# Finer first loads of x, transposes two blocks ahead, and filter tables on another queue in an encoder block on one core

## The chip, the cores and the metric

The kernel runs on one NeuronCore of a Trainium2 chip. The metric is device time in microseconds (us). Three timed runs of the kernel before took 2923.29, 2925.0 and 2925.0 us, median 2925.0. The engines are named as the profile names them: PE (matrix products; PEld its weight loads), DVE (vector), ACT (scalar), POOL (general), and SP, which only issues transfers. SP and ACT issue on hardware queues, POOL on a software queue.

## The reference

One block on x of 512 tokens x 2048 features, float32. Only its start matters here:

```
hn = rmsnorm(x, norm1_w)                     # x * rsqrt(mean(x*x) + eps) * w
proj = hn @ w_in                             # 2048 x 13328
conv_out = depthwise_conv(proj[..., :5120], conv_w, conv_b)     # 3 taps along the tokens
h = sin(f1 * (z @ w1 + b1)); h = sin(f2 * (h @ w2 + b2)); h = h @ w3   # filters of the long convolution
```

Behind it come the long convolutions by spectra (the tables c_dft), a chunked mLSTM in both directions whose gates are 16 columns of proj, the merge of both branches, and a gated feed-forward part.

## The kernel before

Every float32 operand of a product is split into a rounded part h and a remainder l (helper `split_w`, L160 to 166: ACT casts h, DVE subtracts), and a product is three PE passes, h·h, h·l and l·h (`mm3`, L72). Weights come in units of 128 x 4 x 256 (512 KB) through three buffers `wr`, loaded on SP (`load_a`, L154), and are split in two steps of two 128-row blocks each.

x is loaded as token rows (tiles `xt`, 128 tokens each) and must be transposed: for each of 16 blocks of 128 features, four PE transposes fill one PSUM bank (L280), ACT scales it by norm1_w into h (L283) and DVE makes l (L284). Both read norm1_w as a column, from the tile `cols`: conv_w, conv_b, norm1_w and norm2_w are loaded as rows (`rows_a`, `rows_b`, L97 to 102, on ACT's queue), transposed on PE (L105, L106) and copied by DVE (L107). Norm1's factor per token is applied later, after the products: the squares of x run on ACT (L291), their sums become `rstd` and the broadcast row `rbc` (L292 to 295).

The first group of w_in (256 columns, 16 blocks, `group_feat`, L192) is interleaved with this in the code: four blocks are transposed and split, then two steps of the group follow, a step being two blocks' products, 12 on PE (L275 to 287). Behind it come the gates' columns (tiles `wg`, four narrow loads of 128 x 4 x 16, L410 to 437, through the same `wr` and `wh` buffers), the second group, and so on. A side stream runs beside the groups: first `filter_net` (L526), which loads the tables c_dft and zt and the filter net's small weights and vectors on POOL's queue, splits the tables, and computes the net.

The order in the code is not the order of an engine: a scheduler at build time takes instructions from the code by its own estimates of when their operands are ready, and writes an order for each engine. An engine then works strictly in that order, waiting for semaphores. Transfers of the hardware queues take eight completion semaphores in turn, so an issue waits until the transfer eight issues earlier has landed. A buffer is loaded anew when its last readers are done; the pool `ph`, which holds the filter net's small tiles, lies where `xp` (x tiles, rows_a, rows_b) lay.

Of the kernel before, what the change touches and what calls it, by code (L numbers as in the profile page):

```python
# [34 lines left out]
def hybrid_block_kernel(ctx, tc, x, norm1_w, w_in, conv_w, conv_b, filt_w1, filt_b1, filt_freq1,  # L35
# [15 lines left out]

    cp = ctx.enter_context(tc.tile_pool(name="cp", bufs=1))
# [5 lines left out]
    ap = ap_cm.__enter__()  # L58
# [25 lines left out]

    csm = new(cp, "csm", (P, 3 * P + 16))
    nc.sync.dma_start(csm[:, 0:P], c_small[:, 0:P])
    nc.gpsimd.dma_start(csm[:, P:3 * P + 16], c_small[:, P:3 * P + 16])
    ident = csm[:, 0:P]
    triu = csm[:, P:2 * P]
    tril = csm[:, 2 * P:3 * P]  # L90
# [4 lines left out]
    xp_cm = tc.tile_pool(name="xp", bufs=1)  # L95
    xp = xp_cm.__enter__()
    rows_a = new(xp, "rows_a", (120, P))  # L97
    nc.scalar.dma_start(rows_a, conv_w[0].rearrange("k (b p) -> (k b) p", p=P))
    rows_b = new(xp, "rows_b", (72, P))
    nc.scalar.dma_start(rows_b[0:40], conv_b[0].rearrange("(b p) -> b p", p=P))  # L100
    nc.scalar.dma_start(rows_b[40:56], norm1_w[0].rearrange("(b p) -> b p", p=P))
    nc.scalar.dma_start(rows_b[56:72], norm2_w[0].rearrange("(b p) -> b p", p=P))
    cols = new(cp, "cols", (P, 192))
    pt = sd_ps()
    nc.tensor.transpose(pt[:, 0:120], rows_a, ident[0:120, 0:120])  # L105
    nc.tensor.transpose(pt[:, 120:192], rows_b, ident[0:72, 0:72])  # L106
    nc.vector.tensor_copy(cols, pt[:, 0:192])  # L107
    cw = cols[:, 0:120].rearrange("p (k b) -> p k b", k=3)
    cb = cols[:, 120:160]
    n1 = cols[:, 160:176]  # L110
    n2 = cols[:, 176:192]


    def dram(name, shape=(P, L)):
# [39 lines left out]
    def load_a(w, r0, c0, nk=4, ncol=256):  # L154
        n_tile[0] += 1
        raw = wpool[0].tile([P, nk, ncol], F32, tag="wr", name=f"wr_{n_tile[0]}", bufs=3)
        nc.sync.dma_start(raw, w[r0:r0 + nk * P, c0:c0 + ncol].rearrange("(k p) c -> p k c", p=P))
        return raw
# [33 lines left out]
    def group_feat(w, r0, nkb, c0, act, raws=None, ahead=None):  # L192

        ps = [mm_ps(), mm_ps()]
        units = w_units(w, r0, nkb, c0, raws)
        for u in range(0, nkb, 2):
            h, l = next(units) if ahead is None else ahead.get(c0, u)
            for j in range(2):
                for k in range(2):
                    kb = u + k  # L200
                    aH, aL = act[kb]
                    cs = slice(j * P, (j + 1) * P)
                    mm3(ps[j], h[:, k, cs], l[:, k, cs], aH, aL, kb == 0, kb == nkb - 1)
            yield None
        yield ps
# [57 lines left out]


    X = [None] * KB
    ssq_c = new(cp, "ssq_c", (P, 4, 4))
    xt = [[new(xp, f"xt{c}_{tb}") for tb in range(4)] for c in range(4)]
    raws = []
    for c in range(4):
        for tb in range(4):  # L270
            nc.sync.dma_start(xt[c][tb], x2d[tb * P:(tb + 1) * P, c * L:(c + 1) * L])
        if c < 3:
            raws.append(load_a(w_in, c * L, 0))
    first_group = group_feat(w_in, 0, KB, 0, X, raws)
    for c in range(4):  # L275
        for k in range(4):
            kb = 4 * c + k
            ps = sd_ps()
            for tb in range(4):
                nc.tensor.transpose(ps[:, tb * P:(tb + 1) * P], xt[c][tb][:, k * P:(k + 1) * P], ident)  # L280
            h = new(ap, "a", dt=F32R)
            l = new(ap, "a", dt=F32R)
            nc.scalar.activation(h, ps, AF.Copy, scale=n1[:, kb:kb + 1])  # L283
            nc.vector.scalar_tensor_tensor(l, ps, n1[:, kb:kb + 1], h.bitcast(F32), ALU.mult, ALU.subtract)  # L284
            X[kb] = (h, l)
        next(first_group)
        next(first_group)
    for c in range(4):
        for tb in range(4):
            sq = xp.tile([P, L], F32, tag="sq", name=f"sq{c}_{tb}", bufs=2)  # L290
            nc.scalar.activation(sq, xt[c][tb], AF.Square, accum_out=ssq_c[:, tb, c:c + 1])  # L291
    ssq = new(cp, "ssq", (P, 4))  # L292
    nc.vector.tensor_reduce(ssq, ssq_c, mybir.AxisListType.X, ALU.add)
    rstd = rstd_from(ssq, "n1")
# [10 lines left out]
    def gt(dt=F32, shape=(P, L)):  # L305
        t = vt(dt)[:, 0:2, 0:258].rearrange("p b c -> p (b c)")[:, 0:L]
        return t if len(shape) == 2 else t.rearrange("p (b c) -> p b c", b=shape[1])
# [218 lines left out]
    def filter_net():  # L526
        tables = []
        for m in range(4):
            t = gt()
            nc.gpsimd.dma_start(t, c_dft[m])  # L530
            tables.append(t)
        vec = new(ph, "fvec", (P, 4))
        for j, src in enumerate((filt_b1, filt_freq1, filt_b2, filt_freq2)):
            for half in range(2):
                nc.gpsimd.dma_start(vec[half * 64:half * 64 + 64, j:j + 1], src[0].rearrange("(n o) -> n o", o=1))
        w1 = new(ph, "fw1", (33, 2, 64))
        w2 = new(ph, "fw2", (64, 2, 64))
        for half in range(2):
            nc.gpsimd.dma_start(w1[:, half, :], filt_w1[0])
            nc.gpsimd.dma_start(w2[:, half, :], filt_w2[0])  # L540
        zt = gt()
        nc.gpsimd.dma_start(zt[0:33], c_zt)
        yield "pause"
        for m, t in enumerate(tables):
            hh = new(ph, f"dH{m}", dt=F32R)
            ll = new(ph, f"dL{m}", dt=F32R)
            nc.scalar.copy(hh, t)
            nc.vector.tensor_tensor(ll, t, hh.bitcast(F32), ALU.subtract)
            dft.append((hh, ll))
            yield 1  # L550
        def sin_layer(ps, b, fr):
            a = gt()
            nc.vector.tensor_scalar(a, ps, b, fr, ALU.add, ALU.mult)
            n = gt()
            nc.vector.tensor_scalar(n, a, INV2PI, MAGIC, ALU.mult, ALU.add)
            nc.vector.tensor_scalar(n, n, MAGIC, None, ALU.subtract)
            for c in (PI_A, PI_B, PI_C):
                nc.vector.scalar_tensor_tensor(a, n, -c, a, ALU.mult, ALU.add)
            nc.vector.tensor_scalar(a, a, PI_CLAMP, -PI_CLAMP, ALU.min, ALU.max)
            nc.scalar.activation(a, a, AF.Sin)  # L560
            return a
# [12 lines left out]
        nc.vector.tensor_tensor(h2["L"], hh, h2["H"].bitcast(F32), ALU.subtract)  # L574
        yield 4
# [755 lines left out]
    w2 = {t: cm.__enter__() for t, cm in w2_cm.items()}  # L1331
# [42 lines left out]
    xp = ctx.enter_context(tc.tile_pool(name="xd", bufs=1, reuse_waits="tile"))  # L1374
# [49 lines left out]
    for c in range(4):  # L1424
        t = new(xq, "xst")
# [14 lines left out]
    for tb in range(4):  # L1440
        ts = slice(tb * P, (tb + 1) * P)
        for c in range(4):
            ps = mm_ps()
            for k in range(NL):
                mm3(ps, H(k)[0][:, ts], H(k)[1][:, ts], W[(c, k)][0], W[(c, k)][1], k == 0, k == NL - 1)
            t = x2[tb][c]
            nc.vector.scalar_tensor_tensor(t, ps, norm2["r"][:, tb:tb + 1], t, ALU.mult, ALU.add)
            n_tile[0] += 1
            sq = xq.tile([P, L], F32, tag="sq", name=f"sq_{n_tile[0]}", bufs=2)
# [4 lines left out]
        for c in range(4):  # L1454
            t = x2[tb][c]
# [64 lines left out]
```

## Time and profile before

| | |
|---|---|
| timed runs, median | 2925.0 us (2923.29 to 2925.0) |
| profiled execution | 2923.41 us, of it span 2921.3 us |
| mean granted clock | 0.996 |
| PE busy | 2883.2 us, 99% of the span |
| DVE, ACT, POOL busy | 2112.2, 1272.4, 195.5 us |
| moved by DMA | 377.01 MB, mean 129 GB/s |

The span runs from the first to the last instruction that was recorded; the profiled execution's time is 2.1 us more. Busy shares are means over the whole span. A row of a timeline merges like instructions that follow each other; the bracket at its end is idle time of that engine before it, with what ended it.

### The profile page before, as it was taken

The page shows a single profiled execution, that of the slowest core. Times are in us where ns is not written, and L with a number is a line of the kernel's source. Part 1 is how long each engine was busy: PE and PEld are TensorE (multiplying, and loading weights), DVE is VectorE, ACT ScalarE, POOL GpSimd, SP SyncE. Part 2 cuts the span into 40 slices and gives each one's busy share as a digit, 9 for nine tenths or more (in the row PEclk, how much of TensorE's full clock was granted, in tenths as well). Part 3 has the DMA queues.
Part 4 walks back from the last instruction along what each step waited for, and adds up shares of the span by engine and source line. Part 5 has one row for each costly group of instructions (what it writes and reads, how often), then busy time and mean ns, then how long its engine had stood idle before and what let it go on. Part 6 is the DMA issues. An engine that isn't in the chain of part 4 may idle for free.

```text
span 2921.3 us, 48184 instructions
## 1 busy us (share of the span) xinstructions
PE 2883.2 (99%) x18412; PEld 2611.4 (89%) x18412; DVE 2112.2 (72%) x3843; ACT 1272.4 (44%) x2259; POOL 195.5 (7%) x449
## 2 busy tenths in 40 slices
PE   8999999999999999999999999999999999999998
PEld 6788887898889999888889999999999998888886
DVE  6897977889478888554449888888888885233336
ACT  5434354436564455222445444444444444233224
POOL 1101011102210001000110000000000000000000
PEclk9999999999999999999999999999999999999999
DMA  5334334334434444743443334333433336343433
GB/s 177 115 107 133 118 117 138 109 115 139 148 124 130 128 137 137 250 140 98 150 136 116 116 117 127 112 116 118 124 121 113 113 94 223 95 127 117 130 109 130
DMA packets 284161, 377.01 MB, mean 129 GB/s; under 512 B 18013, under 2 KB 221147, under 8 KB 283929
## 3 DMA queue, kind: packets, MB, share of 16 engines
q1 hardware_dynamic: 258976, 296.99, 33.1%
q0 software_dynamic: 23552, 74.74, 7.6%
q8 instruction: 144, 2.36, 0.3%
q10 hardware_dynamic: 1401, 2.20, 0.2%
q14 instruction: 88, 0.72, 0.1%
HBM read 326.67 MB, written 47.20 MB: 128 GB/s over the span
## 4 chain that ended last, share of the span: by engine, by line
PE 93%; DVE 3%; DMA 2%; issue 1%; ACT 1%; POOL 0%; SPq 0%; ACTq 0%; DVEq 0%; POOLq 0%
PE mm L70 67%; PE sd L70 26%; DMA wr<-in_w_down_dram 1%; DVE wl L165 0%; DMA xt<-in_x_dram 0%; DVE st L353 0%; PE sd L703 0%; PE sd L1279 0%; PE sd L280 0%; DVE h L81 0%; DMA g<-d_q 0%; DMA d_yb<-g 0%; DMA g<-d_hy 0%; DVE st L350 0%; DVE T L1307 0%
## 5 line engine op out<-in xcount | busy, mean ns | idle before, releaser
L165 DVE TENSOR_TENSOR wl<-wr,wh 128x512 fp32r<-128x512 f32 x512 | 351.1, 689 | 494.5 <-ACT wh L164 489.1
L164 ACT CAST wh<-wr 128x512 fp32r<-128x512 f32 x512 | 316.8, 622 | 768.8 <-PE mm L70 716.1
L70 PE MATMUL mm<-a,wh 128*128 128x512 f32 (+1 forms) x2136 | 625.6, 376 | 0.4 <-ACT wh L1025 0.4
L70 PE MATMUL mm<-T,h 128*128 128x256 f32 x2592 | 470.4, 284 | 3.9 <-ACT h L1025 3.9
L70 PE MATMUL sd<-T,h 128*128 128x256 f32 x2592 | 468.2, 283 | 0.0
L70 PEld LDWEIGHTS mm<-a,wh 128*128 128x128 f32 x2136 | 387.6, 190 | 70.8 <-issue 3.4
L70 PEld LDWEIGHTS mm<-T,h 128*128 128x128 f32 x2592 | 405.5, 193 | 4.3 <-ACT h L1025 4.3
L70 PEld LDWEIGHTS sd<-T,h 128*128 128x128 f32 x2592 | 404.4, 192 | 0.0
L70 PE MATMUL mm<-a,wl 128*128 128x512 f32 (+1 forms) x1068 | 399.8, 375 | 1.5 <-DVE wl L165 1.0
L70 PE MATMUL mm<-wh,h 128*128 128x512 f32 x1280 | 396.3, 391 | 3.7 <-ACT h L80 3.7
L1025 ACT CAST h<-s 128x512 fp32r<-128x512 f32 x395 | 244.8, 621 | 285.4 <-PE sd L70 141.9
L70 PE MATMUL mm<-T,l 128*128 128x256 f32 x1296 | 367.5, 284 | 0.8 <-DVE l L1026 0.8
L70 PE MATMUL sd<-T,l 128*128 128x256 f32 x1296 | 366.8, 283 | 0.0
L70 PEld LDWEIGHTS mm<-wh,h 128*128 128x128 f32 x1280 | 241.5, 189 | 54.3 <-ACT h L80 3.9
L1026 DVE TENSOR_TENSOR l<-s,h 128x512 fp32r<-128x512 f32 x395 | 270.6, 686 | 12.1 <-ACT h L1025 9.7
L1025 ACT CAST h<-r 128x512 fp32r<-128x512 f32 x285 | 176.8, 620 | 221.4 <-PE mm L70 111.2
L70 PE MATMUL mm<-wh,a 128*128 128x256 f32 (+1 forms) x1152 | 259.7, 319 | 0.0
L70 PEld LDWEIGHTS mm<-T,l 128*128 128x128 f32 x1296 | 249.5, 193 | 1.2 <-DVE l L1026 1.2
L70 PE MATMUL mm<-wl,h 128*128 128x512 f32 x640 | 250.0, 391 | 0.0
L70 PEld LDWEIGHTS sd<-T,l 128*128 128x128 f32 x1296 | 248.8, 192 | 0.0
L70 PEld LDWEIGHTS mm<-a,wl 128*128 128x128 f32 x1068 | 202.2, 189 | 37.3 <-DVE wl L165 1.9
L1026 DVE TENSOR_TENSOR l<-r,h 128x512 fp32r<-128x512 f32 x285 | 192.1, 688 | 51.9 <-ACT h L1025 51.6
(371 smaller groups left out, 4370.2 us busy)
## 6 DMA issues: line engine op xcount, KB each, us to landing
r<-in_w_gate_up_dram SPq DMA_DIRECT2D x176, 512.0 KB, 4.8
wr<-in_w_in_dram SPq DMA_DIRECT2D x144, 512.0 KB, 3.9
wr<-in_w_down_dram SPq DMA_DIRECT2D x88, 512.0 KB, 3.6
r<-in_w_in_dram SPq DMA_DIRECT2D x32, 512.0 KB, 4.8
wr<-in_w_out_dram SPq DMA_DIRECT2D x32, 512.0 KB, 5.4
d_h<-xo POOLq DMA_DIRECT2D x44, 256.0 KB, 2.6
hl<-d_h SPq DMA_DIRECT2D x44, 256.0 KB, 3.5
d_g<-xo POOLq DMA_DIRECT2D x32, 256.0 KB, 3.9
```

The source lines that it names most:

```text
L70: nc.tensor.matmul(o, a, b, start=start, stop=stop)
L164: nc.scalar.copy(h, src)
L165: nc.vector.tensor_tensor(l, src, h.bitcast(F32), ALU.subtract)
L1025: nc.scalar.copy(h, a)
L1026: nc.vector.tensor_tensor(l, a, h.bitcast(F32), ALU.subtract)
```

## The change

Four edits. x is loaded in five pieces of 256, 256, 512, 512 and 512 columns instead of four of 512, the first weights behind the first piece. The loop takes two blocks at a time: both are transposed, then one step of the group's products on the two blocks before them is emitted, then the two new blocks are split. The column constants are divided: norm1, norm2 and conv_b as `rows_b` with norm1 first, transposed after the first two blocks; conv_w as `rows_a`, loaded on SP and transposed after the first group. The loads of `filter_net` and the rest of c_small go from POOL's queue to SP's.

```diff
     nc.sync.dma_start(csm[:, 0:P], c_small[:, 0:P])
-    nc.gpsimd.dma_start(csm[:, P:3 * P + 16], c_small[:, P:3 * P + 16])
...
-    nc.scalar.dma_start(rows_a, conv_w[0].rearrange("k (b p) -> (k b) p", p=P))
     rows_b = new(xp, "rows_b", (72, P))
-    nc.scalar.dma_start(rows_b[0:40], conv_b[0].rearrange("(b p) -> b p", p=P))
-    nc.scalar.dma_start(rows_b[40:56], norm1_w[0].rearrange("(b p) -> b p", p=P))
-    nc.scalar.dma_start(rows_b[56:72], norm2_w[0].rearrange("(b p) -> b p", p=P))
+    nc.scalar.dma_start(rows_b[0:16], norm1_w[0].rearrange("(b p) -> b p", p=P))
+    nc.scalar.dma_start(rows_b[16:32], norm2_w[0].rearrange("(b p) -> b p", p=P))
+    nc.scalar.dma_start(rows_b[32:72], conv_b[0].rearrange("(b p) -> b p", p=P))
...
+    def small_columns():
+        pt = sd_ps()
+        nc.tensor.transpose(pt[:, 120:192], rows_b, ident[0:72, 0:72])
+        nc.vector.tensor_copy(cols[:, 120:192], pt[:, 120:192])
+
+    def conv_columns():
+        nc.sync.dma_start(rows_a, conv_w[0].rearrange("k (b p) -> (k b) p", p=P))
+        pt = sd_ps()
+        nc.tensor.transpose(pt[:, 0:120], rows_a, ident[0:120, 0:120])
+        nc.vector.tensor_copy(cols[:, 0:120], pt[:, 0:120])
...
-    xt = [[new(xp, f"xt{c}_{tb}") for tb in range(4)] for c in range(4)]
+    pieces = [(0, 256), (256, 256), (512, 512), (1024, 512), (1536, 512)]
+    xt = [[new(xp, f"xt{c}_{tb}", (P, n)) for tb in range(4)] for c, (_, n) in enumerate(pieces)]
     raws = []
-    for c in range(4):
+    for c, (c0, n) in enumerate(pieces):
         for tb in range(4):
-            nc.sync.dma_start(xt[c][tb], x2d[tb * P:(tb + 1) * P, c * L:(c + 1) * L])
-        if c < 3:
-            raws.append(load_a(w_in, c * L, 0))
+            nc.sync.dma_start(xt[c][tb], x2d[tb * P:(tb + 1) * P, c0:c0 + n])
+        if c in (0, 2, 3):
+            raws.append(load_a(w_in, len(raws) * L, 0))
...
+    for kb in range(0, KB, 2):
+        blocks = [x_block(kb), x_block(kb + 1)]
+        if kb == 0:
+            small_columns()
+        if kb:
+            next(first_group)
+        for k in range(2):
+            x_split(kb + k, blocks[k])
+    next(first_group)
+    conv_columns()
...
-            nc.gpsimd.dma_start(t, c_dft[m])
+            nc.sync.dma_start(t, c_dft[m])
...
-                nc.gpsimd.dma_start(vec[half * 64:half * 64 + 64, j:j + 1], src[0].rearrange("(n o) -> n o", o=1))
+                nc.sync.dma_start(vec[half * 64:half * 64 + 64, j:j + 1], src[0].rearrange("(n o) -> n o", o=1))
...
-            nc.gpsimd.dma_start(w1[:, half, :], filt_w1[0])
-            nc.gpsimd.dma_start(w2[:, half, :], filt_w2[0])
+            nc.sync.dma_start(w1[:, half, :], filt_w1[0])
+            nc.sync.dma_start(w2[:, half, :], filt_w2[0])
...
-        nc.gpsimd.dma_start(zt[0:33], c_zt)
+        nc.sync.dma_start(zt[0:33], c_zt)
+        nc.sync.dma_start(csm[:, P:3 * P + 16], c_small[:, P:3 * P + 16])
```

`x_block` holds the four transposes of one block and `x_split` the activation and subtraction, as they were in the loop.

PE at the first products, before (`sd` are PSUM banks of transposes, `mm` of products, `xt_N` x's token tiles, `a` the split x, `wh` and `wl` the weights' parts, `csm` holds the identity):

```order
L280 MATMUL sd_199<-csm_72,xt_3_11_164 128x128
L280 MATMUL sd_208<-csm_72,xt_3_11_164 128x128
L280 MATMUL sd_217<-csm_72,xt_3_11_164 128x128
L280 MATMUL sd_226<-csm_72,xt_3_11_164 128x128
L280 MATMUL sd_269<-csm_72,xt_0_12_165 128x128
L70 MATMUL mm_235<-a_204,wh_237 128x512
L70 MATMUL mm_235<-a_205,wh_237 128x512
```

PE at the same place now:

```order
L289 MATMUL sd_201<-csm_72,xt_3_10_158 128x128
L289 MATMUL sd_206<-csm_72,xt_3_10_158 128x128
L289 MATMUL sd_222<-csm_72,xt_0_11_159 128x128
L289 MATMUL sd_227<-csm_72,xt_0_11_159 128x128
L70 MATMUL mm_232<-a_214,wh_234 128x512
L289 MATMUL sd_222<-csm_72,xt_1_12_160 128x128
L289 MATMUL sd_227<-csm_72,xt_1_12_160 128x128
L70 MATMUL mm_232<-a_215,wh_234 128x512
```

Two blocks instead of four stand ahead of the first product, and the second piece's transposes (xt_0_11 to xt_3_14) are interleaved with the first products.

POOL's queue before, from the tables to the last of the filter net's loads (`g` tables and zt, `fvec` vectors, `fw` weights, `gb` the gates' bias):

```order
L530 DMA g_574<-in_c_dft_dram 128x512
...
L542 DMA g_597<-in_c_zt_dram 33x512
L426 DMA gb_665<-in_mlstm_gate_bias_dram 16x1
L535 DMA fvec_582<-in_filt_b_dram 64x1 x2
...
L539 DMA fw_112_591<-in_filt_w_dram 33x64
L540 DMA fw_113_592<-in_filt_w_dram 64x64
```

SP's queue now, from the last weights of the first group (wr_438) to the fifth pair of blocks of the second (wr_780); of the four tables, the four narrow gate loads, the eight fvec and the four fw loads, the first one or two of a kind stand here:

```order
L163 DMA wr_438<-in_w_in_dram 128x4x256
L109 DMA rows_a_79<-in_conv_w_dram 120x128
L163 DMA wr_571<-in_w_in_dram 128x4x16
L551 DMA g_591<-in_c_dft_dram 128x512
...
L563 DMA g_614<-in_c_zt_dram 33x512
...
L163 DMA wr_698<-in_w_in_dram 128x4x256
L163 DMA wr_708<-in_w_in_dram 128x4x256
L556 DMA fvec_599<-in_filt_b_dram 64x1 x2
...
L560 DMA fw_117_608<-in_filt_w_dram 33x64
L561 DMA fw_118_609<-in_filt_w_dram 64x64
...
L664 DMA sg_899<-in_filt_w_dram 64x256 x2
L163 DMA wr_780<-in_w_in_dram 128x4x256
```

The tables now stand behind all of x and the first group's weights, the small loads behind the second group's first two weight loads, and ahead of its third.

PE behind the first group, before (`rb` the rows of the broadcast, `wg` the gates' weights in their four pieces, `wh_682` the second group's first, `g_597` zt; the 32 gate products lie between the rows shown):

```order
L70 MATMUL mm_236<-a_437,wl_460 128x512
L70 MATMUL sd_521<-csm_72,rb_522 128x128
L70 MATMUL mm_553<-a_204,wg_556 128x512
...
L70 MATMUL mm_553<-a_438,wg_651 128x512
L70 MATMUL sd_663<-g_597,fw_112_591 128x512
L70 MATMUL mm_678<-a_204,wh_682 128x512
```

PE behind the first group now:

```order
L70 MATMUL mm_233<-a_460,wl_465 128x512
L111 MATMUL sd_481<-csm_72,rows_a_79 128x120
L70 MATMUL sd_538<-csm_72,rb_539 128x128
L70 MATMUL mm_570<-a_214,wg_573 128x512
...
L70 MATMUL mm_696<-a_214,wh_700 128x512
L70 MATMUL mm_696<-a_215,wh_700 128x512
L70 MATMUL mm_696<-a_214,wl_701 128x512
L70 MATMUL mm_696<-a_218,wh_700 128x512
L70 MATMUL mm_570<-a_420,wg_669 128x512
...
L70 MATMUL mm_570<-a_461,wg_669 128x512
L70 MATMUL sd_681<-g_614,fw_117_608 128x512
```

The transpose of rows_a stands between the group's last product and the broadcast, and four products of the second group (mm_696) stand before the last eight of the gates.

## Rows read from the trace of the kernel before

**Rows 1.** The page, busy time by engine and the chain by engine

```profile
PE 2883.2 (99%) x18412; PEld 2611.4 (89%) x18412; DVE 2112.2 (72%) x3843; ACT 1272.4 (44%) x2259; POOL 195.5 (7%) x449
PE 93%; DVE 3%; DMA 2%; issue 1%; ACT 1%; POOL 0%; SPq 0%; ACTq 0%; DVEq 0%; POOLq 0%
```

**Rows 2.** Busy time by stage: us, busy us (instructions) of each engine, clock, DMA share, GB/s

```profile
0.00:13.80 13.80, 4.87 (x19) 3.24 (x20) 2.23 (x6) 5.47 (x11) 8.94 (x25) 1.00 0.86 277
...
17.00:42.90 25.90, 25.87 (x137) 21.29 (x136) 17.95 (x39) 20.02 (x45) 0.00 (x0) 1.00 0.48 146
```

**Rows 3.** The chain of waits from 0 to 70: start, us, what

```profile
1.51 3.24 DMA rows_b<-in_conv_b_dram
...
4.77 8.86 DMA xt<-in_x_dram
```

**Rows 4.** Timeline, ACT's queue: start, us the issue took, line, transfer

```profile
0.80 0.67 ACTq L98 DMA_DIRECT2D rows_a<-in_conv_w_dram  x1
...
1.83 0.34 ACTq L101 DMA_DIRECT2D rows_b<-in_norm_w_dram  x1
2.20 0.44 ACTq L102 DMA_DIRECT2D rows_b<-in_norm_w_dram  x1
```

**Rows 5.** Timeline of PE, 0 to 24: start, us, instructions merged

```profile
3.05 0.46 PE L105 MATMUL sd<-csm,rows_a 120*128 120x120 f32 x1 [3.05 <-DMA rows_a<-in_conv_w_dram]
...
6.78 0.35 PE L106 MATMUL sd<-csm,rows_b 72*128 72x72 f32 x1 [0.82 <-DMA rows_b<-in_norm_w_dram]
...
13.86 2.05 PE L70 MATMUL mm<-a,wh 128*128 128x512 f32 x4
...
16.98 0.63 PE L70 MATMUL mm<-a,wl 128*128 128x512 f32 x2
17.45 0.62 PE L70 MATMUL mm<-a,wh 128*128 128x512 f32 x2
...
20.64 0.39 PE L70 MATMUL mm<-a,wl 128*128 128x512 f32 x1
20.87 1.80 PE L280 MATMUL sd<-csm,xt 128*128 128x128 f32 x15
```

**Rows 6.** Timeline, ACT and DVE on the first weights

```profile
12.93 0.62 ACT L164 CAST wh<-wr 128x512 fp32r<-128x512 f32 x1
...
13.58 0.69 DVE L165 TENSOR_TENSOR wl<-wr,wh 128x512 fp32r<-128x512 f32 x1
```

**Rows 7.** The page, transfers issued: count, size, median us to landing

```profile
wr<-in_w_in_dram SPq DMA_DIRECT2D x144, 512.0 KB, 3.9
```

**Rows 8.** Timeline, PE's weight loads that waited for DVE, 22 to 38

```profile
22.92 0.19 PEld L70 LDWEIGHTS mm<-a,wh 128*128 128x128 f32 x1 [0.22 <-DVE a L284]
...
30.47 0.19 PEld L70 LDWEIGHTS mm<-a,wh 128*128 128x128 f32 x1 [0.46 <-DVE a L284]
...
37.76 0.19 PEld L70 LDWEIGHTS mm<-a,wh 128*128 128x128 f32 x1 [0.33 <-DVE a L284]
```

**Rows 9.** Timeline of PE: first broadcast product, filter net's first product

```profile
43.12 0.38 PE L70 MATMUL sd<-csm,rb 128*128 128x128 f32 x2
...
51.83 1.12 PE L70 MATMUL sd<-g,fw 33*128 33x512 f32 x2
```

**Rows 10.** Line 642, filter rows on SP: issue ns min/median/max; landing

```profile
L642 SPq DMA_DIRECT2D sg<-in_filt_w_dram x4: 556/586/596, 37.4 to 39.2; - x4
...
DMA to landing us min/median/max: 3.7/3.7/3.7
```

**Rows 11.** Line 535, small loads on POOL: two issues, and landing of all

```profile
8.41 0.52 POOL L535 DMA_DIRECT2D fvec<-in_filt_freq_dram  x1 [1.97 <-DMA g<-in_c_dft_dram]
...
11.64 0.52 POOL L535 DMA_DIRECT2D fvec<-in_filt_b_dram  x1 [0.76 <-DMA g<-in_c_dft_dram]
...
DMA to landing us min/median/max: 5.1/5.3/6.9
```

**Rows 12.** Busy time in a late stretch, columns as in Rows 2

```profile
2426.80:2433.60 6.80, 6.18 (x15) 4.83 (x16) 4.30 (x8) 3.30 (x8) 1.08 (x2) 0.50 0.85 311
```

More of the change, by code (lines that the diff above doesn't have):

```diff
@@ L97, in hybrid_block_kernel @@
     rows_a = new(xp, "rows_a", (120, P))
-    nc.scalar.dma_start(rows_a, conv_w[0].rearrange("k (b p) -> (k b) p", p=P))
     rows_b = new(xp, "rows_b", (72, P))
-    nc.scalar.dma_start(rows_b[0:40], conv_b[0].rearrange("(b p) -> b p", p=P))
-    nc.scalar.dma_start(rows_b[40:56], norm1_w[0].rearrange("(b p) -> b p", p=P))
-    nc.scalar.dma_start(rows_b[56:72], norm2_w[0].rearrange("(b p) -> b p", p=P))
+    nc.scalar.dma_start(rows_b[0:16], norm1_w[0].rearrange("(b p) -> b p", p=P))
+    nc.scalar.dma_start(rows_b[16:32], norm2_w[0].rearrange("(b p) -> b p", p=P))
+    nc.scalar.dma_start(rows_b[32:72], conv_b[0].rearrange("(b p) -> b p", p=P))
     cols = new(cp, "cols", (P, 192))
[L104 to L107, printed above, removed]
+    def small_columns():
[7 more added lines that the diff above has]
+        nc.vector.tensor_copy(cols[:, 0:120], pt[:, 0:120])
     cw = cols[:, 0:120].rearrange("p (k b) -> p k b", k=3)
-    cb = cols[:, 120:160]
-    n1 = cols[:, 160:176]
-    n2 = cols[:, 176:192]
+    n1 = cols[:, 120:136]
+    n2 = cols[:, 136:152]
+    cb = cols[:, 152:192]
     def dram(name, shape=(P, L)):
@@ L265, in hybrid_block_kernel @@
     X = [None] * KB
-    ssq_c = new(cp, "ssq_c", (P, 4, 4))
-    xt = [[new(xp, f"xt{c}_{tb}") for tb in range(4)] for c in range(4)]
+    ssq_c = new(cp, "ssq_c", (P, 4, 5))
+    pieces = [(0, 256), (256, 256), (512, 512), (1024, 512), (1536, 512)]
+    xt = [[new(xp, f"xt{c}_{tb}", (P, n)) for tb in range(4)] for c, (_, n) in enumerate(pieces)]
     raws = []
-    for c in range(4):
+    for c, (c0, n) in enumerate(pieces):
         for tb in range(4):
-            nc.sync.dma_start(xt[c][tb], x2d[tb * P:(tb + 1) * P, c * L:(c + 1) * L])
-        if c < 3:
-            raws.append(load_a(w_in, c * L, 0))
+            nc.sync.dma_start(xt[c][tb], x2d[tb * P:(tb + 1) * P, c0:c0 + n])
+        if c in (0, 2, 3):
+            raws.append(load_a(w_in, len(raws) * L, 0))
@@ L274, in hybrid_block_kernel @@
     first_group = group_feat(w_in, 0, KB, 0, X, raws)
[L275 to L287, printed above, removed]
@@ L288, in hybrid_block_kernel, with x_block, x_split @@
-    for c in range(4):
+    def x_block(kb):
+        ps = sd_ps()
+        c = max(i for i, (c0, _) in enumerate(pieces) if c0 <= kb * P)
+        k0 = kb * P - pieces[c][0]
+        for tb in range(4):
+            nc.tensor.transpose(ps[:, tb * P:(tb + 1) * P], xt[c][tb][:, k0:k0 + P], ident)
+        return ps
+    def x_split(kb, ps):
+        h = new(ap, "a", dt=F32R)
+        l = new(ap, "a", dt=F32R)
+        nc.scalar.activation(h, ps, AF.Copy, scale=n1[:, kb:kb + 1])
+        nc.vector.scalar_tensor_tensor(l, ps, n1[:, kb:kb + 1], h.bitcast(F32), ALU.mult, ALU.subtract)
+        X[kb] = (h, l)
@@ L289, in hybrid_block_kernel @@
+    for kb in range(0, KB, 2):
[8 more added lines that the diff above has]
+    conv_columns()
+    for c, (_, n) in enumerate(pieces):
         for tb in range(4):
             sq = xp.tile([P, L], F32, tag="sq", name=f"sq{c}_{tb}", bufs=2)
-            nc.scalar.activation(sq, xt[c][tb], AF.Square, accum_out=ssq_c[:, tb, c:c + 1])
+            nc.scalar.activation(sq[:, 0:n], xt[c][tb], AF.Square, accum_out=ssq_c[:, tb, c:c + 1])
```

## The prediction

> **What bounds the kernel now.** I read the page's busy shares and chain first, then the busy time of the first 43 us by stages, then chain, timeline and queues of that stretch. The reader is to see in the first that TensorE (PE) is busy for 99% of the span and carries 93% of the chain that ended last [rows 1]: what comes to PE earlier is worth its full length, and what other engines do counts only where PE waits. The stages show where it does: from 0 to 13.8 us PE is busy 4.87 us, from 17.0 to 42.9 us 25.87 of 25.90 [rows 2]. So the change can win in the first 14 us, and a little at the block boundaries after them. The chain there runs through transfers: conv_b's bias rows, 3.24 us, then an x tile whose issue on SP had waited for them [rows 3]. SP waits because each transfer takes one of eight completion semaphores and may start only when the transfer eight earlier has landed.
>
> By the order of instructions everything from PE's 488th row on stands as before, so the change is a shift of what follows plus what the first 488 rows gain or lose. All times below are of the profiled execution, span 2921.3 us and 2923.41 us in all; the median of the timed runs, 2925.0, lies 1.6 above it, and I apply the sum to the median.
>
> **The start.** Before, PE's first product stands at 13.86 us [rows 5], behind 1 MB of x, the first weights, and on POOL's queue 1 MB of tables that share the DMA engines. The engines move 277 GB/s on average up to 13.8 us [rows 2], so about 3.8 MB pass before that product; in the new order the first two x pieces and the first weights are 1.5 MB, and the tables are gone. Bandwidth is then not what decides, a landing is: the first weights take the semaphore of conv_b's rows, which the ACT queue now issues third. Third there was an issue at 1.83 us [rows 4]; with conv_b's own 3.24 us [rows 3] it lands at 5.07. Bounds: the first small transfer went from 0.80 to its consumer at 3.05, 2.25 us; the last from 2.20 to 6.78, 4.58 us [rows 4, 5]; so 4.08 to 6.41. A 512 KB weight transfer lands 3.9 us after its issue [rows 7]: 8.97 (7.98 to 10.31). ACT rounds the weights in 0.62 us [rows 6] and the first product can start: 9.59 (8.60 to 10.93). That is **4.27 us earlier** (2.93 to 5.26).
>
> x's second piece follows the weights on the same queue, in 128 KB tiles; PE takes them between the first products, and the low parts of the weights (0.69 us on DVE, [rows 6]) end inside that work. I cost both at nothing: the cover is the interleaved transposes, and without it one 0.69 us is lost.
>
> **Block boundaries.** Before, four blocks were transposed at once and then multiplied; at three starts of such a batch PE's weight loads wait for DVE's low parts, 0.22, 0.46 and 0.33 us [rows 8]. Now the next two blocks are transposed ahead of the current two blocks' products, so these waits fall: **1.01 us** (0 to 1.01). On the other side 54 of the 64 transposes stand behind the first product where 47 did; 7 at 0.12 us (15 take 1.80, [rows 5]) cost **0.84**. ACT could be late next: from the first weights' cast to the last activations of blocks 6 and 7 its order holds 20 instructions, of 0.62 us or less for the most part, so 12.4 us, done at about 21.4. PE comes to those blocks about 23.1 (three pairs at 12 x 0.228 + 8 x 0.12 = 3.7 us, plus some 2.5 us for the clock). The cover is 1.7 us.
>
> **The clock.** The first seven products, 13.86 to 16.98, go at 0.446 us each; 14 products from 17.45 to 20.64 at 0.228 [rows 5]. The first pace is that of the lower level, 1.2 GHz, though the granted clock is written as 1.00 for the whole stretch [rows 2]. The rise came 3.12 us after the first product. Starting at 9.59, it comes between 12.71 (the same distance) and 16.98 (the same time of the program): the extra low-pace time of 0 to 4.27 us costs half of itself, 0 to 2.13. Nothing says which, so I take the middle, **1.07**.
>
> The Trainium skill, TensorE: Matmul & The Clock Gate, section on what is actually happening, says that activity releases the low default clock, and that the monitor's period runs free of the kernel's start. By that rule the rise may fall anywhere between the two bounds, and the sum moves by at most the 2.13; the single rise in this trace neither confirms nor denies it.
>
> **Behind the first group.** The conv columns' transpose moves to the end of the group: 0.12. The last gate weights (the fourth narrow piece of w_in) now come late enough that the scheduler puts four products of the second group before them; DVE has row-broadcast and eviction work in between. The trace has no such wait; between none and one more DVE instruction (0.69, [rows 6]) I take the half: 0.35. Together **0.47** (0.12 to 0.81).
>
> **A new wait.** fvec, the first of the filter net's small tiles, lies where rows_a lay, so its load waits until the conv columns are transposed, at the end of the first group; before, rows_a was read at 3.05 us [rows 5]. Behind it on SP stand 11 further small loads, then filter rows and the weights of the second group's fifth pair of blocks. PE needs the second fw1 (the 11th) for the filter net's first product. That product follows the group's end by 8.71 us (43.12 to 51.83, [rows 9]), now plus 0.47 and the four early products, 0.91: the group ends at 43.12 - 4.27 - 1.01 + 0.84 + 1.07 = 39.75, the product is due at 49.84. The loads: start 39.87, 11 issues, a landing. The nearest rows are the filter rows' loads on the same queue, 0.586 us an issue and 3.7 to land [rows 10]: 39.87 + 6.45 + 3.7 = 50.02, **0.18 late**. Bounds: ACT's small issue of 0.34 [rows 4] and 2.25 to land give 45.9, no wait; POOL's pace for these same loads, 1.08 apart (8.41 to 11.64 in three steps), and 5.3 to land [rows 11] give 57.05, 7.2 late. I take 0.18 for the queue being the same. The weights behind are due some 9 us after that product and are covered.
>
> The Trainium skill, DMA: Bandwidth & Descriptors, section on the anatomy of one DMA, speaks against this move: a transfer has a fixed cost of about 2 us, mostly for confirming that it landed. If these went one after the other, an estimate by that figure is 22 us for the eleven, and PE would wait 12. The filter rows' four loads, issued 0.6 us apart and each landing after 3.7 [rows 10], overlap, so here only the last one's landing counts.
>
> Moving the tables off POOL costs nothing there: POOL is waited for by nobody in this stretch. The four tables and zt are needed at the end of the first group and are issued behind the last x piece, some 15 us ahead of it. The squares are 20 instead of 16, of the same columns; ACT's cover above holds them.
>
> **Sum.** 4.27 + 1.01 - 0.84 - 1.07 - 0.47 - 0.18 = 2.7 us earlier: the profiled execution 2920.7, the median **2922.3**.
>
> **Rivals.**
> - *The small loads hold PE up (slower).* PE works in order, so a late fw1 stops everything behind. It takes the place of the whole gain once the loads end 2.7 us later than forecast, 11 issues at 0.83 us, and it is over 0.2% slower from 8.6 later. At POOL's pace: 7.2 late, 2.7 + 0.2 - 7.2 = -4.3, so 2929.3. For it: the same loads were spaced so. Against: there each waited for a table of 256 KB before it [rows 11]; on SP nothing as large is in front but one weight piece.
> - *The start is hidden.* conv_b lands at its late bound (first product 10.93), the block waits return as waits for ACT, the clock rises at 16.98: 2.93 - 0.84 - 1.47 - 0.47 - 0.18 = 0, so 2925.0. For it: small transfers took up to 4.58 us. Against: those shared the engines with POOL's tables, which have gone.
> - *The low-clock stretches fall otherwise (faster).* Far behind the change PE runs at half clock after waits, as from 2426.8 to 2433.6 with 6.18 us busy [rows 12]; shifted, such a stretch may not come: 3.09 us more, 2919.2, and 2916.6 with the early bounds of the start. For it: the skill's rule above would make each run draw anew. Against: the timed runs of before lie within 1.7 us of each other. The reverse, one more stretch, ends at 2925.4.
>
> **How the numbers follow.** Forecast 0.62, small loads 0.10, hidden start 0.12, clock stretches 0.16. The sum's own bounds without the new wait reach from 2919.7 to 2925.4; with half of each outer rival the range is 2918.5 to 2927.0. 0.2% (5.85 us) is about what a measurement of this kernel can tell from no change: under 2919.15 are two thirds of the clock case and a twentieth of the forecast, 0.13; above 2930.85 the far part of the small loads, 0.06; the rest, 0.81, is no change.
>
> **What would show it.** The first product near 9.6 us, its pace doubling between 12.7 and 17; no weight load waiting for DVE's low parts up to 40; the first group's end near 39.8; the filter net's first product near 50 with at most 1 us idle before it. The forecast is wrong if the first weights' cast starts after 10.5, if PE waits over 1 us for fw or for ACT before 50, or if PE's waits behind 100 us differ by more than the shift.

## The result

The changed kernel takes 2905.68 us (median of five runs, 2904.16 to 2908.01), the kernel before in the same comparison 2925.0 (2922.8 to 2929.75): a ratio of 0.9937, 95% interval 0.9927 to 0.9948. That is some 18 us faster; the forecast was 2.7 us, and its range reached down to 2918.5. The span of the profiled execution fell from 2921.3 to 2903.9, by 17.4 us.

In the profiled executions only 4 of the 17.4 us come from the start, where the change was made. The others arise between 840 and 2430 us, in products whose order is the same in both kernels (the last row of PE that differs lies at 117 us). They come from one line that the prediction did not weigh: `ssq_c` grew from 4 x 4 to 4 x 5 numbers, and every tile behind it moved by 32 bytes in SBUF. The spacing of TensorE's products, from 120.0 to 118.3 ns here, depends on where the moving operand (the one of 256 columns) lies relative to the stationary one (the 128 x 128 weights that PEld loads).

### The profile page after: what moved, and what is told of

It reads as the page before. It is cut to its first block, busy times and chain, and to the rows that moved or that the text cites. A ratio compares the mean times of both kernels' runs of the same rounds, so it can differ in the third digit from the quotient of the medians.

```text
span 2903.9 us, 48189 instructions
## 1 busy us (share of the span) xinstructions
PE 2869.5 (99%) x18412; PEld 2595.7 (89%) x18412; DVE 2106.6 (73%) x3844; ACT 1274.0 (44%) x2267; POOL 186.2 (6%) x431
## 4 chain that ended last, share of the span: by engine, by line
PE 93%; DVE 3%; DMA 2%; issue 2%; ACT 1%; POOL 0%; SPq 0%; DVEq 0%; POOLq 0%; ACTq 0%
PE mm L70 66%; PE sd L70 26%; DMA wr<-in_w_down_dram 1%; DVE wl L171 0%; DVE st L374 0%; PE sd L289 0%; PE sd L725 0%; PE sd L1301 0%; DMA bt<-d_o 0%; DVE st L371 0%; DVE h L81 0%; DMA xt<-in_x_dram 0%; DMA g<-d_q 0%; DMA g<-d_hy 0%; DVE T L1329 0%
## 5 line engine op out<-in xcount | busy, mean ns | idle before, releaser
L70 PE MATMUL mm<-T,h 128*128 128x256 f32 x2592 | 463.8, 282 | 3.9 <-ACT h L1047 3.9
L70 PE MATMUL sd<-T,h 128*128 128x256 f32 x2592 | 461.5, 281 | 0.0
L70 PEld LDWEIGHTS mm<-T,h 128*128 128x128 f32 x2592 | 398.5, 189 | 4.4 <-ACT h L1047 4.4
L70 PEld LDWEIGHTS sd<-T,h 128*128 128x128 f32 x2592 | 397.2, 189 | 0.0
```

## The profile after

The page's busy times, to be read beside [rows 1]: PE is busy 13.7 us less with the same 18412 products, so most of the gain is not idle time that went away.

```profile
PE 2869.5 (99%) x18412; PEld 2595.7 (89%) x18412; DVE 2106.6 (73%) x3844; ACT 1274.0 (44%) x2267; POOL 186.2 (6%) x431
```

Where the gain arises is read from groups of products that both kernels have: duration (least, median, most, ns), then first and last start (us). Before:

```profile
L70 PE MATMUL sd<-sg,dH x192: 277/283/386, 111.8 to 571.2; 128*128 128x256 f32 x192
L70 PE MATMUL sd<-T,h x2592: 283/283/283, 879.9 to 2423.3; 128*128 128x256 f32 x200
L70 PE MATMUL mm<-y,wh x256: 389/389/389, 1256.6 to 1343.2; 128*128 128x512 f32 x128
L70 PE MATMUL mm<-wh,h x1280: 387/389/796, 2427.4 to 2865.5; 128*128 128x512 f32 x183
```

After:

```profile
L70 PE MATMUL sd<-sg,dH x192: 277/283/387, 108.8 to 567.1; 128*128 128x256 f32 x192
L70 PE MATMUL sd<-T,h x2592: 277/281/285, 874.4 to 2406.5; 128*128 128x256 f32 x200
L70 PE MATMUL mm<-y,wh x256: 395/396/397, 1249.3 to 1338.5; 128*128 128x512 f32 x128
L70 PE MATMUL mm<-wh,h x1280: 388/389/796, 2410.5 to 2848.1; 128*128 128x512 f32 x183
```

Subtract the starts: the changed kernel is 3.0 us ahead at 112 (4.0 at 117, where the last reordered rows end), 4.1 at 571, 5.5 at 880, 7.3 at 1257, only 4.7 at 1343, 16.8 at 2423 and 17.4 at 2866. The lead grows where products of `T` run, 256 columns wide (`T` are the moving operands of the two stages that the code calls Winograd: the earlier makes the gates of the merge, the later the gated feed-forward), and shrinks by 2.6 over the products of `y`, 512 columns wide. The median durations say the same: T,h 283 to 281 ns, y,wh 389 to 396.

Two stretches show the pace without idle time or a change of clock, before and then after (length, then busy us and count of PE, PEld, DVE, ACT, POOL, then clock, DMA share, GB/s):

```profile
1270.00:1330.00 60.00, 60.00 (x266) 49.70 (x265) 34.69 (x54) 19.40 (x33) 0.00 (x0) 1.00 0.47 146
1600.00:1900.00 300.00, 300.00 (x2503) 300.00 (x2502) 265.82 (x462) 141.36 (x238) 8.13 (x15) 1.00 0.39 119
```

```profile
1270.00:1330.00 60.00, 60.00 (x259) 48.31 (x258) 36.40 (x57) 18.77 (x32) 0.00 (x0) 1.00 0.40 125
1600.00:1900.00 300.00, 300.00 (x2537) 300.00 (x2536) 267.37 (x467) 143.17 (x241) 8.67 (x16) 1.00 0.38 120
```

PE never pauses, the granted clock is 1.00 in all four, and still 2537 products fit where 2503 did, while 259 of the wide ones fit where 266 did. Worked out from the starts of single products: before, 7340 of the 7352 T products of the later Winograd stage start exactly 120 ns after one another; after, their mean is 118.33. 7352 x 1.67 ns are 12.3 us. In the earlier Winograd stage 2659 products, of `T` and `a`, go from 119.99 to 118.89, 2.9 us; 384 of y go from 226.67 to 233.34, 2.6 us lost. With 4.1 from the start that is 16.7 of the 17.4. The waits of PE that the profile names behind 100 us come to 19.1 us before and 17.9 after; the remaining 0.7 can lie there.

The start itself, PE's timeline of the changed kernel, to be read beside [rows 5, 9]:

```profile
8.55 0.69 PE L289 MATMUL sd<-csm,xt 128*128 128x128 f32 x2 [1.96 <-DMA xt<-in_x_dram]
8.89 0.79 PE L70 MATMUL mm<-a,wh 128*128 128x512 f32 x1
...
12.47 0.49 PE L70 MATMUL mm<-a,wl 128*128 128x512 f32 x1
12.79 0.62 PE L70 MATMUL mm<-a,wh 128*128 128x512 f32 x2
13.25 0.39 PE L70 MATMUL mm<-a,wl 128*128 128x512 f32 x1
...
38.68 0.39 PE L70 MATMUL sd<-csm,rb 128*128 128x128 f32 x2
...
48.20 1.12 PE L70 MATMUL sd<-g,fw 33*128 33x512 f32 x2
```

The first product starts at 8.89 (before 13.86), the pace doubles near 12.7, the broadcast stands at 38.68 (43.12) and the filter net at 48.20 (51.83).

## The experiments

Theory A: the addresses set the later pace. Theory B: the edits themselves do (queues, order, what the other engines do meanwhile). The addresses are those of the built programs. In the four shifts of the kernel before, the order of instructions and every PSUM address are those of before; 3922 of 5583 tiles in SBUF lie 32, 64, 96 or 128 bytes further, the others where they lay. Pools grow from both ends of SBUF: wr, wh, wl, the `a` tiles, T in `ts` and `t3`, and the weights h2 and l2 of the later Winograd stage lie on the left behind `cp`, with ssq_c in it; y, T in `tp`, and the extra weights h and l of the earlier Winograd stage lie on the right and stay. The distance below is that of T in `tp` from h2 modulo 512, a weight row having 128 x 4 bytes. The kernel before, run beside each group, took 2926.41 (shift32, noshift, shift64, shift96), 2925.19 (shift128, after64, best2) and 2924.36 us (best3); the ratios are to these.

| kernel | distance | products, 1600 to 1900 | us | ratio to before, interval |
|---|---|---|---|---|
| before | 256 | 2503 | 2925.0 | 1 |
| changed | 224 | 2537 | 2905.68 | 0.9937 (0.9927 to 0.9948) |
| shift32 | 224 | 2537 | 2912.02 | 0.9950 (0.9938 to 0.9963) |
| noshift | 256 | 2503 | 2918.35 | 0.9976 (0.9966 to 0.9986) |
| shift64 | 192 | 2611 | 2887.84 | 0.9870 (0.9855 to 0.9885) |
| shift96 | 160 | 2549 | 2913.47 | 0.9954 (0.9941 to 0.9966) |
| shift128 | 128 | 2526 | 2917.63 | 0.9975 (0.9965 to 0.9984) |
| after64 | 192 | 2611 | 2878.32 | 0.9842 (0.9829 to 0.9856) |
| best2 | 448 | 2630 | 2861.60 | 0.9789 (0.9775 to 0.9802) |
| best3 | 448 | 2630 | 2855.70 | 0.9782 (0.9753 to 0.9811) |

**shift32**, the shift alone:

```diff
-    ssq_c = new(cp, "ssq_c", (P, 4, 4))
+    ssq_c = new(cp, "ssq_c", (P, 4, 5))
...
-    nc.vector.tensor_reduce(ssq, ssq_c, mybir.AxisListType.X, ALU.add)
+    nc.vector.tensor_reduce(ssq, ssq_c[:, :, 0:4], mybir.AxisListType.X, ALU.add)
```

> The kernel before, with ssq_c allocated as (P,4,5) as in the changed kernel and read as before: nothing but the addresses of the tiles behind it changes, by 32 bytes. Theory A (the late gain comes from where the tiles lie): the start takes as long as before, the Winograd products with 256 columns (mm<-T,h) go from 120.0 ns apart to 118 to 119, the branch stage's products (mm<-y,wh) from 227 to 235, and the time falls by about 14 us, to 2910 to 2914. Theory B (the late gain comes from the edits to queues and order): no change, 2924 to 2926, products 120.0 ns apart.

It took 2912.02 us, and its stretches are those of the changed kernel:

```profile
1270.00:1330.00 60.00, 60.00 (x259) 48.31 (x258) 34.67 (x53) 19.24 (x33) 0.00 (x0) 1.00 0.45 144
1600.00:1900.00 300.00, 300.00 (x2537) 300.00 (x2536) 268.37 (x469) 143.96 (x242) 8.65 (x16) 1.00 0.38 120
```

The counts are 259 and 2537 again, with not one of the written edits in it. Theory B falls for the late gain. By the timed runs the shift alone is worth 14.4 us, by the spans of the profiled executions 10.5.

**noshift**, the edits without the shift:

```diff
-    ssq_c = new(cp, "ssq_c", (P, 4, 5))
+    hold = new(cp, "hold", (P, 16))
+    nc.gpsimd.memset(hold, 0.0)
+    ssq_c = new(xp, "ssq_c", (P, 4, 5))
```

> The changed kernel with ssq_c moved into the pool xp and 64 bytes held in its place (a small memset on POOL), so that every tile of the later stages lies at its address of before. Theory A: only the gain of the start is left, some 4 us: 2920 to 2922, with 120.0 ns between the Winograd products. Theory B: the whole gain stays, 2905 to 2907.

2918.35 us, 8.1 below the kernel before and 2 below what was expected; the late stretch is that of before:

```profile
1600.00:1900.00 300.00, 300.00 (x2503) 300.00 (x2502) 266.02 (x462) 141.16 (x238) 8.65 (x16) 1.00 0.38 118
```

In its trace the lead over before is 3 us from 300 to 800 us, what the forecast said of the whole change, and 4.7 at the end, where two stretches at the 1.2 GHz level have been half as long: the granted clock of 840 to 860 is 0.91 here and 0.83 before. The timed runs say the same: the mean granted clock is 0.997 in six of its eight runs and in two of the twelve of before, the means of these clocks differ by 0.0011, and 0.0011 of the span is, as an estimate, 3 of the 8.1 us. So the edits without the shift are worth 3 to 5 us, and shorter stretches at half clock the rest; why these are shorter here is open. The first row is of noshift, the second of before:

```profile
840.00:860.00 20.00, 17.30 (x125) 16.64 (x126) 16.84 (x29) 9.43 (x17) 0.00 (x0) 0.91 0.60 185
```

```profile
840.00:860.00 20.00, 15.15 (x98) 14.15 (x98) 13.42 (x22) 7.19 (x14) 0.54 (x1) 0.83 0.60 196
```

**shift64, shift96, shift128**, as shift32 with ssq_c of 4 x 8, 4 x 10 and 4 x 12:

> The kernel before with ssq_c as (P,4,8): the tiles behind it move by 64 bytes. Theory A with the parity of 32-byte steps as its rule (what counts is whether stationary and moving operand lie alike modulo 64): 2924 to 2926, products 120.0 ns apart. Rival C (any other distance between the two pools helps): faster, near 2911. Theory B: 2924 to 2926.

> The kernel before with ssq_c as (P,4,10): the tiles behind it move by 96 bytes. Theory A with the rule modulo 64: as the shift by 32, 2910 to 2914, Winograd products at 118 to 119 ns, branch products at 235. Rival C' (only a distance of 32 does it): 2924 to 2926. Theory B: 2924 to 2926.

> The kernel before with ssq_c as (P,4,12): the tiles behind it move by 128 bytes. Theory A with the rule that the runs so far give (the pace of the products goes by the distance of moving and stationary operand modulo 128: 120.0 ns at 0, 114.1 at 64): 120.0 ns again, 2924 to 2928. Rival C (a longer period, or every distance between the pools but none is better): 114 to 118 ns, below 2915.

The middle one came as theory A had it (2913.47 us; 117.8 ns where 118 to 119 were expected). The others refute its rules: a shift by 64 gives the largest gain of all, 38.6 us, which no theory had, and a shift by 128 does not bring 120.0 ns back but a mean of 118.9. What stays is that the distance decides, and not by a simple rule. The stretch of shift64, then that of shift128:

```profile
1600.00:1900.00 300.00, 300.00 (x2611) 300.00 (x2611) 274.37 (x483) 147.51 (x248) 8.65 (x16) 1.00 0.39 124
```

```profile
1600.00:1900.00 300.00, 300.00 (x2526) 300.00 (x2524) 267.47 (x467) 143.38 (x241) 8.13 (x15) 1.00 0.38 119
```

The absolute place counts for little: the 768 T products of the earlier Winograd stage whose two operands lie on the left, and so moved together by 32, 64 or 96 bytes, stand 119.7, 120.0 and 119.9 ns apart, as 120.0 before.

**after64**, the changed kernel with ssq_c of 4 x 8:

> The changed kernel with ssq_c as (P,4,8): its tiles lie as in the shift by 64. Theory A: the start's gain of 4 to 7 us beside the placement's 38.6: 2880 to 2884, Winograd products of the last Winograd stage at 114 where T is on the right. Theory B (the edits themselves have a share in the late gain): below 2876.

2878.32 us, 1.7 below that. Placement and start add up by the timed runs: 38.6 (shift64) and 8.1 (noshift) against 46.9 here. By the spans of the profiled executions the start's share is smaller, 5.7 (2876.2 against 2881.9 of shift64). For the changed kernel the two parts, 14.4 and 8.1, come to more than its 19.3 measured in another comparison, so the start's share is known to a few us only.

**best2 and best3**, built on after64, set each kind of product to the distance that suits it:

```diff
-        h = wpool[0].tile(shape, F32R, tag="wh", name=f"wh_{n_tile[0]}", bufs=WB[0])
+        h, l = wslot("wh", f"wh_{n_tile[0]}", off, k), wslot("wl", f"wl_{n_tile[0]}", off, k)
...
+        t = wp.tile([P, 544], F32R, tag=tag, name=name, bufs=4)
+        return at(t, 16 if off else 0 if slots[tag] % 2 else 32, k)
...
-                hl = new(pool, "T", (P, 2, 256), F32R)
+                hl = at(new(pool, "T", (P, 544), F32R), 16, 2) if pool is not tp else new(pool, "T", (P, 2, 256), F32R)
```

`at` takes 512 elements of a longer tile from an offset; best2 has 528 elements and offsets 0 and 16 in `wslot`, best3 the rows above; y in py is treated alike.

> As the run before it, and every other product with 256 columns set 64 bytes (modulo 128) apart, every one with 512 columns at distance 0: tiles of wh and wl are 64 bytes longer and used from byte 0 or 64, those of y and of T in t3 from byte 64. Theory A: 924 products from t3 at 114 instead of 118, 3 us; 768 T and 1032 a of the merge stage and 1152 wh and wl of the narrow token groups at 113.5 instead of 120, 19 us; 384 of y at 227 instead of 233, 2.5 us: 25 us below the run before it, 2855 to 2860. Rival D (the pace belongs to which pool's side the operands are on, not to the distance): as the run before it.

2861.60 us, 17 below after64 where 25 were expected. The T and `a` products of the merge stage did what was expected (113.4 ns). Two thirds of them have both operands on the left, where only their distance has changed, so the side is not what counts, and rival D falls. The others fell short: the narrow token groups came to 116.6 instead of 113.5, those from t3 to 116.2 instead of 114, y to 231.3 instead of 227. And the tiles of 2112 bytes put many wide products at 128 and 384, and those cost: 2642 of `a` at 230.65 instead of 227.93, 7 us. Here distances alternate from product to product, and a product's own distance no longer gives its pace: y takes 230.7 to 231.6 ns at each of 0, 128, 256 and 384.

> As best2, with the tiles of wh, wl and y in steps of 2176 and 2304 bytes, so that every product with 512 columns is again at a distance of 0 modulo 256 and every one with 256 columns at 64 modulo 128 (rb moves out of the pool cp to make room). Theory A: 2707 products a at 231.7 instead of 234.1, 6.5 us, 384 of y at 227 instead of 231.3, 1.7 us, half of the 768 wh at 114 instead of 117.6 or more, 1 to 3 us: 2849 to 2854. Rival E (for 512 columns only the start decides, and what differed in best2 was something else): as best2, 2860 to 2863.

2855.70 us over six runs (2854.38 to 2881.64, the one far value widens the interval), 1.7 above the range. The wide products are back at 227.9 and, for y, 226.66, so rival E falls; the narrow token groups stay at 116.8. The rows show y's stretch with 267 products (before: 266), beside 2630 narrow ones, and a stretch at half clock that its profiled run has at 52 and no other has:

```profile
52.30:59.10 6.80, 6.80 (x20) 5.50 (x20) 4.89 (x15) 2.13 (x3) 1.40 (x3) 0.50 0.81 260
1600.00:1900.00 300.00, 300.00 (x2630) 300.00 (x2629) 275.07 (x483) 150.20 (x252) 7.59 (x14) 1.00 0.39 124
1270.00:1330.00 60.00, 60.00 (x267) 49.67 (x266) 37.02 (x57) 19.51 (x34) 0.00 (x0) 1.00 0.36 115
```

best3 beats both kernels, by 69 us the one before.

**bench**, products alone:

```diff
+    def block(n, m, stats, count=96):
...
+        for i in range(count):
+            o = (i % 2) * 256 if n < 512 else 0
+            s = stats[i % len(stats)]
+            nc.tensor.matmul(ps[:, 0:n], s[:, (i // 2) % 4, :], m[:, o:o + n], start=i == 0, stop=i == count - 1)
...
+    for n in (256, 512):
+        for d in range(0, 257, 32):
+            block(n, M[d], [s0])
```

> Products alone: everything of the block is left out, and blocks of 96 products with nothing to wait for run one behind the other, each block with its own moving tile (ma to mi: 0, 32, ... 256 bytes from the stationary's place modulo 256), with 256 columns and then with 512, then three blocks of 128 columns (0, 64, 128), and two whose stationary tiles alternate between 0 and 64. Theory A: with 256 columns 120 ns at 0 and 256, near 119 at 128, 117 to 119 at odd multiples of 32, 113 to 115 at 64 and 192; with 512 columns 227 at 0 and 256 and 232 to 235 elsewhere. Rival D (it is which pool, or what else the engines do meanwhile): the same pace in every block of one width. Alternating stationaries: if it is the next weight load beside the current columns that collides, the two kinds of product differ by the next one's place, else by their own.

PE's timeline, one row for each block of 96; the next row's start less this one's, by 96, is the pace. The first row has the busy times of the whole stretch (PE, PEld, DVE, ACT, POOL, clock, DMA share, GB/s):

```profile
70.00:442.00 372.00, 370.95 (x2222) 328.04 (x2220) 12.73 (x24) 0.00 (x0) 0.00 (x0) 1.00 0.00 1
...
72.86 11.68 PE L84 MATMUL mm<-ma,sa 128*128 128x256 f32 x96
84.37 11.47 PE L84 MATMUL sd<-mb,sa 128*128 128x256 f32 x96
95.68 11.47 PE L84 MATMUL mm<-mc,sa 128*128 128x256 f32 x96
106.99 11.67 PE L84 MATMUL sd<-md,sa 128*128 128x256 f32 x96
118.50 11.56 PE L84 MATMUL mm<-me,sa 128*128 128x256 f32 x96
129.89 11.43 PE L84 MATMUL sd<-mf,sa 128*128 128x256 f32 x96
141.16 11.07 PE L84 MATMUL mm<-mg,sa 128*128 128x256 f32 x96
152.07 11.52 PE L84 MATMUL sd<-mh,sa 128*128 128x256 f32 x96
163.42 11.68 PE L84 MATMUL mm<-mi,sa 128*128 128x256 f32 x96
174.94 21.95 PE L84 MATMUL sd<-ma,sa 128*128 128x512 f32 x96
196.72 22.57 PE L84 MATMUL mm<-mb,sa 128*128 128x512 f32 x96
219.13 22.15 PE L84 MATMUL sd<-mc,sa 128*128 128x512 f32 x96
...
353.19 21.93 PE L84 MATMUL sd<-mi,sa 128*128 128x512 f32 x96
374.95 10.83 PE L84 MATMUL mm<-ma,sa 128*128 128x128 f32 x96
```

Beside DVE's copy after each block nothing else runs in this stretch, and the pace still differs by block: rival D falls here too. From ma to mb are 11.51 us, 120 ns each; from mg to mh 10.91, 113.6; mb's wide block takes 22.41 where ma's takes 21.78 and mi's 21.76. Three points of the expectation failed: with 256 columns 64 (117.8 ns) and 96 (120.0), with 512 columns 64 (228.9). The table has the distances modulo 512 (every second moving tile begins half a weight row later), for the bench the mean without the first dozen products of a block, for the kernels the mean at full clock of the products between the two sides; 64 occurs in best2 and best3 alone, among other distances:

| distance mod 512 | 0, 256 | 64 | 128 | 160 | 192 | 224 | 288 | 320 | 352 | 416 | 448 | 480 |
|---|---|---|---|---|---|---|---|---|---|---|---|---|
| 256 columns, bench, ns | 120.0 | 117.8 | 118.7 | | 113.3 | | 117.8 | | 120.0 | 117.4 | | 118.3 |
| 256 columns, kernels, ns | 120.0 | 113.0 to 118.0 | 118.9 | 117.4 | 114.1 | 118.2 | 117.3 | 113.3 | 119.2 | | 113.5 | |
| 512 columns, bench, ns | 226.7 | 228.9 | 233.4 | | 233.4 | | 233.3 | | 233.3 | 234.3 | | 233.4 |

Where a distance stands in both rows and all products of the kind share it, the two agree to 0.9 ns. The period is not settled: modulo 256 the bench's 64 (117.8) and the kernels' 320 (113.3) would have to be alike, but 64 itself took 113.0 to 118.0 among other distances. With 128 columns the three blocks (0, 64, 128) go at 111.6 to 111.7. The blocks with alternating stationaries (distances 0 and 192; 118.3 and 232.4 ns) differ neither cleanly by the own nor by the next one's place, and lie nearer to the slower of the two distances. Neighbours do count: 1845 T products at distance 0 that stand among others at 192 in the later stage of shift64 take 117.8 instead of 120.0. How is left open.

**st_four and st_pool**, parts of the start undone in the changed kernel:

```diff
-    pieces = [(0, 256), (256, 256), (512, 512), (1024, 512), (1536, 512)]
+    pieces = [(0, 512), (512, 512), (1024, 512), (1536, 512)]
```

> The changed kernel with x in four pieces of 512 columns, the first weights again behind the first of them; the transposes stay two blocks ahead, addresses of the later stages as in the changed kernel. If the smaller first pieces carry the start's gain (the step of the forecast: the first weights land earlier): first product near 11 to 12 instead of 8.9, and the later stages 2 to 3 us later than in the changed kernel. If the two-blocks-ahead order carries it: first product at 9 to 10, less than 1 us later.

The first product stands at 10.93 and waits for ACT on the weights; the stages from 140 to 600 us stand 1.1 to 1.7 us later, less than the 2 to 3 expected: of the 4 us the pieces carry little over one. The first product came near its expectation of 11 to 12. There is one run, 2906.13 us.

```profile
10.93 1.20 PE L70 MATMUL mm<-a,wh 128*128 128x512 f32 x4 [0.58 <-ACT wh L170]
```

```diff
-            nc.sync.dma_start(t, c_dft[m])
+            nc.gpsimd.dma_start(t, c_dft[m])
...
-        nc.sync.dma_start(zt[0:33], c_zt)
+        nc.gpsimd.dma_start(zt[0:33], c_zt)
```

(and the small loads and the rest of c_small likewise)

> The changed kernel with the loads of the filter net and the rest of c_small on POOL's queue as before. The forecast holds the move to SP for nearly free: 0.2 us late at the filter net's first product. If so, this run's later stages stand within 0.5 us of the changed kernel's. If the move carries a part of the start's gain (less beside the first loads of x), they stand 1 us or more later.

The second holds: the first product moves to 12.02 and the stages from 140 to 600 us stand 2.9 to 3.1 us later (one run, 2908.22 us).

```profile
11.66 0.69 PE L290 MATMUL sd<-csm,xt 128*128 128x128 f32 x2 [2.70 <-DMA xt<-in_x_dram]
12.02 0.80 PE L70 MATMUL mm<-a,wh 128*128 128x512 f32 x1
```

With the tables on POOL's queue PE waits 2.70 us at 11.66 for x's second piece, with them on SP 1.96 at 8.55. So about 3 of the start's 4 us hang on this move and little over one on the pieces, by one run each. That it is the tables which delay x is argued from the two waits; the small loads and the rest of c_small moved back with them. The order two blocks ahead and the divided columns were not undone by themselves.

## Why the prediction was wrong

**The step that failed** is the sentence that by the order of instructions everything from PE's 488th row on stands as before, so that the change is a shift of what follows plus what the first rows gain. Behind 117 us the order is the same; the pace is not. Between 840 and 2430 us the same products took 12.6 us less (15.2 less for the narrow ones, 2.6 more for y), and shift32 shows the same counts from the address shift alone. The last sign named in the prediction, waits behind 100 us that differ by more than the shift, could not show this: the waits hardly differ (19.1 and 17.9 us), and in the two stretches above there is none.

**The forecast's own terms** fared better: it gave 2.7 us, noshift's lead at 300 us is 3, the changed kernel's 4. That the sum comes near is in part luck, since its first term has the wrong wait and one gain is missing.
- First product: forecast 9.59 (8.60 to 10.93), measured 8.89. The reason was another: the first weights' issue did not wait for conv_b. In the built program it is the ninth transfer of the hardware queues and takes the semaphore of the first, norm1's rows; conv_b's goes to the last tile of x's second piece. SP's rows show the weights' issue at 3.14, where the prediction had 5.07, and their cast starts at 8.22 (forecast 8.97). The chain to the first product runs through x's second piece, which had been costed at nothing.

```profile
3.14 0.43 SPq L163 DMA_DIRECT2D wr<-in_w_in_dram  x1
3.62 4.92 SPq L279 DMA_DIRECT2D xt<-in_x_dram  x8
```

```profile
3.62 4.89 DMA xt<-in_x_dram
```

```profile
8.22 1.14 ACT L170 CAST wh<-wr 128x512 fp32r<-128x512 f32 x2
```

- The tables' move was priced as a cost of nothing and nowhere as a gain, and bandwidth was called what does not decide. st_pool shows about 3 us there.
- The clock's rise came near 12.7 us, the early bound. That is 3.6 to 3.9 us behind the first product where it was 3.12 before; by the forecast's own rule half of the difference, an estimated 0.3 of the 1.07 us, was lost.
- Block boundaries: no weight load waits for DVE up to the group's end any more, as forecast [rows 8]. The group ends at least 1.07 us earlier than the 39.75 forecast: the broadcast behind it starts at 38.68.
- The new wait: fvec's issues begin at 38.9 and fw's last at 45.6; fvec's landing takes 2.3 us, not 3.7, and the filter net starts at 48.20, behind the four early products, without a wait on SP that shows. The transfers overlap (12 issues between 38.9 and 46.1), so the serial estimate of 22 us was rightly set aside. The fixed cost of about 2 us that it rests on stands in the Trainium skill (DMA: Bandwidth & Descriptors, section on the anatomy of one DMA) for the software queue; here the same kind of load on SP's hardware queue landed after 2.3 us.

```profile
DMA to landing us min/median/max: 2.3/2.3/2.3
```

- Rivals: the small loads were not late, the start not hidden. The one on the clock stretches named the right side but the wrong cause for this kernel: it has the stretches of before, as the one at 2409 to 2416, which brings 2402 to 2422 to 0.83 (beside [rows 12]). In noshift the rival's mechanism did show, with some 3 us:

```profile
2402.00:2422.00 20.00, 16.42 (x82) 14.01 (x81) 11.05 (x21) 7.27 (x13) 3.21 (x6) 0.83 0.86 296
```

## What to carry to other kernels

When a change alters the size of any tile, list which addresses move with it, before arguing that the untouched stages only shift: in the profiled executions here 32 bytes were worth three times the written edits (12.6 and 4.1 us). Where PE is busy throughout, look at the spacing of like products, not at waits; if narrow products stand at a stiff 120.0 ns, a few dozen bytes of padding between the moving and the stationary tile are the cheapest experiment there is. Choose the distance for each width by measuring: 192 bytes take products of 256 columns from 120.0 to 113.3 ns and those of 512 from 226.7 to 233.4. Give it to every product of a run, since mixed distances kept only part of the gain (best2).

## What the runs showed of the hardware

- The pace of products with their weight loads depended on the distance in SBUF between moving and stationary operand (counted modulo 512 here; the period is not settled): 113.3 to 120.0 ns with 256 columns, 226.7 to 234.3 with 512; with 128 columns the three distances tried give 111.6 to 111.7. Of the slowest distances for 256 columns (0, 256, 352) the first two are the fastest for 512.
- In a run of products with mixed distances a product's own distance does not give its pace: y at 0 took 231.6 ns in best2 and 226.7 in best3.
- It needs no other engine's work beside the products and no transfer (bench), and the granted clock was 1.00 in the stretches compared. Why it is so, whether the reads of columns and of weights meet in the memory, no run tells.
- Tiles that are all multiples of 512 bytes long keep every pair within one side at one distance, so in these programs one odd tile of 64 or 96 bytes set the distance of some 5500 products between the sides in the later Winograd stage.
